# Up product of the ConvFFN without plain pairs: two products of 16 pairs run first, in PSUM banks of their own

## The chip, the cores and the metric

One core of a Trainium2 chip runs one layer of a streaming encoder in one launch. The metric is the device time of that launch in microseconds, as the median of three runs. The clock that was granted to TensorE in the profiled execution is 0.997 of full speed, so throttling plays no part here.

## The reference, cut to what matters

The layer handles T = 1056 tokens (1024 of a prompt and 32 of a decode group) at D_MODEL = 1024, with D_FF = 2816. The part that matters is the ConvFFN and the product just ahead of it:

```python
mix = (sigmoid(ga) * (oa @ w_br_a) + sigmoid(gb) * (ob @ w_br_b)) @ w_out
x = x + rms_norm(mix, g_post_mix)
f, conv_new = conv_ffn(rms_norm(x, g_pre_ffn), ...)

def conv_ffn(h, conv_s0, w_up, conv_w, conv_b, w_down):
    a, g = jnp.split(h @ w_up, [D_FF], axis=-1)             # w_up: 1024 x 5632
    gx = jnp.concatenate([conv_s0, g], axis=1)
    gc = conv_b + sum(conv_w[i] * gx[:, i:i + T] for i in range(3))
    return (gelu(gc) * a) @ w_down, gx[:, T:]
```

All arithmetic is float32.

## The kernel before, in words

Features lie on the 128 partitions and tokens along the free axis, so an activation of 1024 features is eight slices of 128. A float32 product is made of three matmuls in a faster format (fp32r in the names): each factor is split into a high half, copied by ScalarE (whi, mh/hh), and a low half, that is the factor less its high half, made by VectorE (wlo, ml/hl). High times high, high times low and low times high are added in PSUM. Raw weights are loaded by DMA on SP's queue; results go out by POOL's queue.

**Order.** From the out product to the end of the plain pairs the code stands in a `manual_schedule`: PE, DVE and ACT issue their work as it is written. Behind it a scheduler chooses the order by data and buffers; weights (`plus`, `weight`) have high priority there. Each engine works its queue in order.

**PSUM.** `repsum((mm, one, two))` deals the eight banks out: so many single banks called mm, so many called one, so many pairs of banks called two. The call ahead of the branch products deals (4, 4, 0), and this holds for the stages branch (L1653 and on: L1664 reads a product into ev, with the low half oa3l of an activation made at L236 by VectorE), out and plain up. The next call, (0, 0, 4), holds for the pairs that take seven products.

**Out and norm.** The product with w_out goes over three chunks of 352 tokens, eight slices each. ScalarE squares and scales each slice (sq, z), VectorE sums the squares (accz, L1866). `norm_steps` is a generator that does the norm of a chunk: fold accz (L1744) and split it into two halves y (L1755, L1756), sum over partitions by TensorE, inverse root by VectorE, scale z (L1778), add the residual, and do the same once more for the norm ahead of the up product (L1781 scales z, L1810 makes the low half in ml/hl, and the rows are also stored in DRAM as d_hn). The numbers in OUT_STEPS and UP_STEPS say how many steps of the generator stand behind each product. The norm of chunk 2, the last, is spread over the up product that follows.

**Up.** The 44 slices of w_up are 22 pairs (f), of a slice of a and one of g. Pairs 0 to 3 are plain: two halves by three chunks by 24 matmuls of 352 columns (L230 to L232). Each of the other 18 takes a 2x2 scheme with seven products in place of eight: features and tokens are halved (528 tokens a half, one and two), the two slices of the weights make the other way to halve, and a product is 24 matmuls of 264 columns (L2048 to L2050) into a pair of banks. In the order of the program, with tN the differences of quarters of the activation, sN those of weights:

```python
X  = a11*b11 -> p1 (ScalarE, L2065)     Y = s2*t2      -> c12 = p1 + Y (L2103)
Z  = s1*t1   -> q = p1 + Z (L2107)      X += a12*b21   -> c11 (ScalarE, L2109)
Y += s3*t3   -> last quarter = q + Y (L2058 to L2060)
Z += s4*b22  -> c12 += Z (L2115)        Y += a22*t4    -> c21 = p1 + Y (L2117)
```

`plus` (L2031) makes the weight sums ws, `weight` their halves (L2038, L2039). The quarters t1 to t4 are made during the plain pairs and after (`quarter_sums`, `quarter_third`, `quarter_last`) from rows of d_hn that are read back, t2 by way of DRAM.

**Behind a pair.** `activate` does the convolution (L1899 on ScalarE, L1901 and L1902 on VectorE, in the single buffer gc), gelu (L1906), the product with a (L1911, L1913, into av), and sm, the sum of both token halves (L1921), which it puts in gc. POOL stores av and sm in d_b for the down product; from pair 11 on these stores accumulate. The last pair (21) runs its products in another order. The down product (L2510 to L2512) follows.

Of the kernel before, what the change touches and what calls it, by code (L numbers as in the profile page):

```python
# [1 line left out]

# [94 lines left out]
UP_PLAIN = 4  # L97

THIRD = ((0, 0), (1, 0, 0), (0, 1, 0), (0, 0, 1), (1,), ())
# [4 lines left out]
OUT_STEPS = (1, 1, 1, 2, 2, 2, 2, 1)  # L104
UP_STEPS = (0, 1, 2, 2, 2, 1, 2, 2, 2)
# [8 lines left out]
def emit(tc, a):  # L114
# [1525 lines left out]
    repsum((MODE, 8 - MODE, 0))  # L1640
# [108 lines left out]
    def norm_steps(tmp, c, z, acc, g, resid, keep, g_next, dst, spill=None):  # L1749
# [58 lines left out]
        def low_half(i):  # L1808
            nh, nl = dst(i)
            ve.tensor_tensor(nl, zs[i], nh, op=ALU.subtract)  # L1810

        for i in range(KT // 2):
            times(i, g_next, rstd(s))
            if spill is not None:
                po.dma_start(both(spill, i), zs[i])
            ac.activation(dst(i)[0], zs[i], AF.Copy)
            if i:
                low_half(i - 1)
            yield
# [17 lines left out]
    wup = {}  # L1837

    def up_weights(f, j):
        n = f + FT * (1 - j)  # L1840
        wup[f, j] = weights(a["w_up"][n], ve) if f == 0 else split_into(uw, a["w_up"][n], 8)
# [3 lines left out]
    for c in range(NC):  # L1845
# [3 lines left out]
        for n in range(KT):  # L1849
# [3 lines left out]
            if c == 0:  # L1853
                out_weights(n + 2)
            else:
                norm_part(OUT_STEPS[n])
            if c == NC - 1 and n in (4, 5):
                up_weights(0, n - 4)
# [8 lines left out]
        if c == 0:  # L1867
# [3 lines left out]
                          lambda i, s=s: [t[:, 2 * i : 2 * i + 2, s] for t in (hh, hl)], d_hn)  # L1871
        next(norm)
        for i in rest or ():
            pass
# [20 lines left out]
    def activate_steps(f, gx, av):  # L1895
# [24 lines left out]
        both, sm = av.rearrange("p (q t) -> p q t", q=2), gc[:, :HT]  # L1920
# [10 lines left out]
    def plain_out(gx, av, j, s, ps):  # L1931
        if j:
            ac.activation(av[:, s], ps, AF.Copy)
        elif s.stop <= NP:
            ac.activation(gx[:, s.start + 2 : s.stop + 2], ps, AF.Copy)
        else:
            n = NP - s.start
            ac.activation(gx[:, s.start + 2 : NP + 2], ps[:, :n], AF.Copy)
            ac.activation(gx[:, NP + 4 :], ps[:, n:], AF.Copy)

    def up_plain():
        bufs = {}
        steps = [(0, 0, 0), (0, 1, 0), (0, 0, 1), (0, 1, 1)]
        steps += [(f, j, c) for cs in ((0, 1), (2,)) for f in range(3) for j in range(2) for c in cs if f or c == 2]

        for i, (f, j, c) in enumerate(steps):
            if (f, 0) not in bufs:
                bufs[f, 0] = up_buffers(f)
            gx, av = bufs[f, 0]
            s = chunk(c)  # L1950
            ps = ps_mm()[:, : s.stop - s.start]
            hi, lo = wup[f, j]
            product(ps, hi, lo, [(k, k) for k in range(KT)], lambda k: hh[:, k, s], lambda k: hl[:, k, s])
            if i == 14:
                wup[3, 0] = weights(a["w_up"][3 + FT], ve)
            if i < 9:
                norm_part(UP_STEPS[i])
            elif i >= 11:
                next(rest, None)
            if i % 2 == 0 and 1 + i // 4 < 3:  # L1960
                up_weights(1 + i // 4, i // 2 % 2)
            if i == 8:
                rest = plain_rest(bufs)
            plain_out(gx, av, j, s, ps)
        return bufs


    XS = {}
    d_t2 = tl(dram, [HK, P, HT], tag="d_t2")

    def quarter_rows(k):
        b = [tl(sh, [P, T], tag="hn", bufs=2) for i in range(2)]
        dma.dma_start(b[0], d_hn[k])
        dma.dma_start(b[1][:, two], d_hn[k + HK, :, two])
        return b[0][:, one], b[0][:, two], b[1][:, two]

    def quarter_split(n, k, t):
        h, l = (v[:, k] for v in XS[n])
        ac.activation(h, t, AF.Copy)
        ve.tensor_tensor(l, t, h, op=ALU.subtract)  # L1980

    def quarter_sums():
        for n in ("t1", "t2"):
            XS[n] = [tl(sp, [P, HK, HT], F32R, tag=n + x, bufs=1) for x in "hl"]
        for k in range(HK):
            b11, b12, b22 = quarter_rows(k)
            t1, t2 = [tl(sh, [P, HT], tag="xs", bufs=2) for i in range(2)]
            ve.tensor_tensor(t1, b12, b11, op=ALU.subtract)
            ve.tensor_tensor(t2, b22, t1, op=ALU.subtract)
            dma.dma_start(d_t2[k], t2)  # L1990
            quarter_split("t1", k, t1)
            quarter_split("t2", k, t2)
            yield

    def quarter_third():
        XS["t3"] = [tl(sw, [P, HK, HT], F32R, tag="t3" + x) for x in "hl"]
        for k in range(HK):
            t = tl(sh, [P, T], tag="hn", bufs=2)
            dma.dma_start(t[:, one], d_hn[k, :, two])
            dma.dma_start(t[:, two], d_hn[HK + k, :, two])  # L2000
            yield
            ve.tensor_tensor(t[:, one], t[:, two], t[:, one], op=ALU.subtract)
            quarter_split("t3", k, t[:, one])
            yield

    def quarter_last():
        XS["b11"] = [t[:, up1, one] for t in (hh, hl)]
        XS["b21"] = [t[:, up2, one] for t in (hh, hl)]
        XS["b22"] = [t[:, up2, two] for t in (hh, hl)]
        XS["t4"] = [t[:, up1, two] for t in (hh, hl)]  # L2010
        for k in range(HK):
            t = tl(sh, [P, T], tag="hn", bufs=2)
            dma.dma_start(t[:, one], d_t2[k])
            dma.dma_start(t[:, two], d_hn[HK + k, :, one])
            ve.tensor_tensor(t[:, one], t[:, two], t[:, one], op=ALU.subtract)
            quarter_split("t4", k, t[:, one])
# [4 lines left out]
    def up_strassen(f):  # L2021
        raw = [tl(wp, [P, KT, P], tag="raw", bufs=2), tl(wp, [P, KT, P], tag="raw", bufs=2) if f == UP_PLAIN else sw_raw()[:, : KT * P].rearrange("p (k c) -> p k c", c=P)]
# [5 lines left out]
        def plus(x, y, o, e):  # L2028
            t = tl(sw, [P, HK, P], tag="ws", bufs=3)
# [32 lines left out]
        X = ps_pair()  # L2062
        X_ = X[:, :, :HC]
        mul(X, weight(a11, WL_ENG[0]), "b11", True, True)
        ac.activation(p1, X_, AF.Copy)  # L2065
# [37 lines left out]
        ve.tensor_tensor(c12, p1, Y_, op=ALU.add)  # L2103
        Z = ps_pair()
# [3 lines left out]
        mul(X, weight(a12, WL_ENG[3]), "b21", False, True)  # L2108
        ac.activation(c11, X_, AF.Copy)  # L2109
# [10 lines left out]
    sp = sh = None  # L2120


    def plain_rest(bufs):
        nonlocal sp, sh
        zp.release()
        sp = pool("sp", side="right")
        for x in ("t1h", "t1l", "t2h", "t2l"):
            tl(sp, [P, HK, HT], F32R, tag=x, bufs=1)
        sh = pool("sh", side="right")
        yield from quarter_sums()  # L2130
        activate(0, *bufs[0, 0])
        yield
# [706 lines left out]
```

## Time and profile before

| | |
|---|---|
| median of 3 runs | 1900.38 us (1898.66 to 1902.38) |
| the profiled execution: span | 1898.7 us; no other time is shown for it |
| TensorE matmul (PE), weight load (PEld) | 1864.9 us (98%), 1828.7 us (96%) |
| VectorE (DVE) | 1232.9 us (65%) |
| ScalarE (ACT) | 956.5 us (50%) |
| GpSimd (POOL) | 211.6 us (11%) |
| memory traffic | 166 GB/s over the span |

All views come from one profiled execution. Times are microseconds from the start of the span. In a list by time a row gives start, duration, engine, line, operation, output and inputs, sizes, and in brackets how long the engine stood idle ahead of it and what released it. In a table of stretches each engine has its busy time and its count of instructions. In a list by group "573/578/584" are the shortest, mean and longest duration in nanoseconds, followed by the time of the first and the last. In a list of transfers a row ends with the KB of one and the median time from issue to landing. TensorE's matmuls are pipelined, so that their durations overlap.

### The profile page before, as it was taken

To read this page: it belongs to the slowest core of one execution; us is meant where nothing else is said; L and a number is where in the kernel's file an instruction comes from. 1 tells how busy PE (TensorE), PEld (TensorE's weight loads), DVE (VectorE), ACT (ScalarE), POOL (GpSimd) and SP (SyncE) were. 2 spreads that over 40 slices of the span, in tenths; PEclk is the share of its full clock that TensorE was granted. 3 is DMA by queue.
4 is the path that set the end of the run, shared out by engine and by line. 5 is a ranking of instruction groups with operands and counts; after the bars stand their busy time and mean duration, and the time that the engine had idled before them with its cause. 6 is when DMAs were issued, how large, how long until landed. Compare 5 with 4: busy or idle time off the path is not lost.

```text
span 1898.7 us, 34427 instructions
## 1 busy us (share of the span) xinstructions
PE 1864.9 (98%) x13616; PEld 1828.7 (96%) x13616; DVE 1232.9 (65%) x2325; ACT 956.5 (50%) x2028; POOL 211.6 (11%) x374
## 2 busy tenths in 40 slices
PE   8999999999999999999999999999999999999996
PEld 8999999999999999999999999999999999999996
DVE  6955544566655766675544776777776775558776
ACT  7545335666666676563324544443433344555555
POOL 0000001010000111011210121111122110000112
PEclk9999999999999999999999999999999999999998
DMA  7223326233315656678633446334445468987646
GB/s 282 82 101 108 108 82 195 66 98 85 103 49 143 164 150 172 180 225 284 232 114 116 145 154 217 135 133 140 138 109 133 109 188 295 299 276 240 235 147 109
DMA packets 112702, 300.89 MB, mean 158 GB/s; under 512 B 12756, under 2 KB 36636, under 8 KB 111900
## 3 DMA queue, kind: packets, MB, share of 16 engines
q1 hardware_dynamic: 83084, 205.95, 34.0%
q0 software_dynamic: 28016, 88.05, 17.1%
q10 hardware_dynamic: 1440, 4.69, 0.6%
q8 instruction: 107, 1.75, 0.4%
q14 instruction: 55, 0.45, 0.1%
HBM read 201.20 MB, written 114.09 MB: 166 GB/s over the span
## 4 chain that ended last, share of the span: by engine, by line
PE 84%; DVE 6%; ACT 5%; DMA 3%; issue 2%; POOL 0%; SPq 0%; ACTq 0%; DVEq 0%; POOLq 0%
PE two L2048 6%; PE mm L232 6%; PE mm L230 6%; PE two L2049 6%; PE two L2050 6%; PE mm L231 6%; PE mm L821 5%; PE mm L823 5%; PE mm L822 5%; PE two L618 4%; PE two L619 4%; PE two L620 4%; PE two L2511 3%; PE two L2512 3%; PE two L2510 3%
## 5 line engine op out<-in xcount | busy, mean ns | idle before, releaser
L821 PE MATMUL mm<-xh,whi 128*128 128x352 f32 x696 | 238.1, 342 | 0.4 <-ACT ev L714 0.4
L823 PE MATMUL mm<-xh,wlo 128*128 128x352 f32 x696 | 225.1, 323 | 0.0
L822 PE MATMUL mm<-xl,whi 128*128 128x352 f32 x696 | 224.6, 323 | 0.0
L2512 PE MATMUL two<-d,wlo 128*128 128x264 f32 x616 | 175.4, 285 | 0.8 <-DVE wlo L2247 0.8
L2511 PE MATMUL two<-d,whi 128*128 128x264 f32 x616 | 174.9, 284 | 0.9 <-DVE d L2198 0.8
L2510 PE MATMUL two<-d,whi 128*128 128x264 f32 x616 | 174.4, 283 | 0.0
L2050 PE MATMUL two<-mh,wlo 128*128 128x264 f32 x576 | 163.3, 285 | 0.0
L2048 PE MATMUL two<-mh,whi 128*128 128x264 f32 x576 | 161.7, 285 | 1.5 <-DVE gx L2060 1.5
L2049 PE MATMUL two<-ml,whi 128*128 128x264 f32 x576 | 163.0, 284 | 0.0
L821 PEld LDWEIGHTS mm<-xh,whi 128*128 128x128 f32 x696 | 131.2, 189 | 3.2 <-ACT ev L714 0.7
L822 PEld LDWEIGHTS mm<-xl,whi 128*128 128x128 f32 x696 | 131.3, 189 | 0.3
L823 PEld LDWEIGHTS mm<-xh,wlo 128*128 128x128 f32 x696 | 130.6, 188 | 0.0
L2511 PEld LDWEIGHTS two<-d,whi 128*128 128x128 f32 x616 | 115.9, 188 | 1.5 <-DVE d L2198 1.5
L2512 PEld LDWEIGHTS two<-d,wlo 128*128 128x128 f32 x616 | 115.6, 188 | 1.0 <-DVE wlo L2247 1.0
L2510 PEld LDWEIGHTS two<-d,whi 128*128 128x128 f32 x616 | 116.3, 189 | 0.0
L2048 PEld LDWEIGHTS two<-mh,whi 128*128 128x128 f32 x576 | 107.5, 188 | 1.7 <-DVE gx L2060 1.7
L2050 PEld LDWEIGHTS two<-mh,wlo 128*128 128x128 f32 x576 | 108.5, 188 | 0.2 <-DVE wlo L2039 0.2
L2049 PEld LDWEIGHTS two<-ml,whi 128*128 128x128 f32 x576 | 108.4, 188 | 0.0
L958 ACT ACTIVATE s<-s,sm 128x640 f32<-128x640 f32 (+5 forms) x72 | 50.6, 703 | 93.4 <-DVE sm L957 93.4
L618 PE MATMUL two<-th,whi 128*128 128x264 f32 x320 | 90.8, 284 | 0.0
L619 PE MATMUL two<-tl,whi 128*128 128x264 f32 x320 | 90.8, 284 | 0.0
L620 PE MATMUL two<-th,wlo 128*128 128x264 f32 x320 | 90.6, 284 | 0.0
(630 smaller groups left out, 5870.7 us busy)
## 6 DMA issues: line engine op xcount, KB each, us to landing
raw<-in_w_in SPq DMA_DIRECT2D x52, 512.0 KB, 3.7
d_b<-av POOLq DMA_DIRECT2D x33, 528.0 KB, 4.2
d_ws<-in_w_down POOLq DMA_DIRECT2D x24, 704.0 KB, 6.5
uraw<-d_b SPq DMA_DIRECT2D x32, 528.0 KB, 5.7
raw<-in_w_up SPq DMA_DIRECT2D x27, 512.0 KB, 3.6
wraw<-d_ws SPq DMA_DIRECT2D x16, 704.0 KB, 5.6
d_b<-gc POOLq DMA_DIRECT2D x11, 792.0 KB, 5.8
sraw<-in_w_up SPq DMA_DIRECT2D x17, 512.0 KB, 4.6
```

Source lines behind the costliest of these rows:

```text
L618: pe.matmul(ps[:, j, :HC], w[0][:, k], x[0](k, s), start=st, stop=False, skip_group_check=True)
L619: pe.matmul(ps[:, j, :HC], w[0][:, k], x[1](k, s), start=False, stop=False, skip_group_check=True)
L620: pe.matmul(ps[:, j, :HC], w[1][:, k], x[0](k, s), start=False, stop=sp_, skip_group_check=True)
L821: pe.matmul(ps, wh, h[:, k, s], start=(k == 0), stop=False)
L822: pe.matmul(ps, wh, l[:, k, s], start=False, stop=False)
L823: pe.matmul(ps, wl, h[:, k, s], start=False, stop=(k == cnt - 1))
L2048: pe.matmul(ps[:, j, :HC], w[0][:, k], x[0][:, k, s], start=st, stop=False, skip_group_check=True)
L2049: pe.matmul(ps[:, j, :HC], w[0][:, k], x[1][:, k, s], start=False, stop=False, skip_group_check=True)
L2050: pe.matmul(ps[:, j, :HC], w[1][:, k], x[0][:, k, s], start=False, stop=sp_, skip_group_check=True)
L2510: pe.matmul(o, wh, xh_[:, s], start=(k == 0 and p in (0, 4, 5)), stop=False, skip_group_check=True)
L2511: pe.matmul(o, wh, xl_[:, s], start=False, stop=False, skip_group_check=True)
L2512: pe.matmul(o, wl, xh_[:, s], start=False, stop=(k == HD - 1 and p in (3, 4, 6)), skip_group_check=True)
```

## The change

- No pair is plain any more; all 22 take seven products.
- For 16 pairs (AHEAD) the two products that go into X run in a stage of their own, ahead of all others: `up_ahead` makes a11\*b11, copies it to av as p1 (L2013), adds a12\*b21 in the same bank, copies that as c11, and POOL stores both in DRAM (d_e). Later `up_strassen` reads p1 and c11 back (SP's queue) and does the other five products. Pairs 4, 8, 12, 16, 20 and 21 do all seven there.
- The first four products of each kind in this stage are cut at the half of the tokens' half (264 columns), so that they can start before the norm of chunk 2 is done; `norm_steps` of chunks 1 and 2 run on behind them, with new OUT_STEPS and UP_STEPS.
- PSUM is dealt (3, 1, 2) from the branch products on, in place of (4, 4, 0): two pairs of banks for the new stage, and single banks for its first products.
- The high and low halves of the activation are only made for what the scheme uses (`used`).
- Rows of d_hn for the quarters t1 to t4 are loaded straight into the tiles that will hold their low halves (tXl) and summed from there during the new stage (`quarter_sums`, L1972 on ScalarE); t2 no longer goes by DRAM.
- sm has a tile of its own (L1941, one buffer), except for the last pair. p1 has two buffers in place of one.
- Raw weights of the new stage lie in the buffers raw and gx (`up_load`, `up_split`).

```diff
-UP_PLAIN = 4
+AHEAD = (0, 1, 2, 3, 5, 6, 7, 9, 10, 11, 13, 14, 15, 17, 18, 19)
-UP_STEPS = (0, 1, 2, 2, 2, 1, 2, 2, 2)
+UP_STEPS = (1, 1, 1, 1, 0, 1, 0, 1) + (1,) * 12
...
-    repsum((MODE, 8 - MODE, 0))
+    repsum((3, 1, 2))
...
-        both, sm = av.rearrange("p (q t) -> p q t", q=2), gc[:, :HT]
+        both, sm = ..., gc[:, :HT] if f == FT - 1 else tl(sw, [P, HT], tag="sm", bufs=1)
...
+    def ahead_product(X, i, p, js=(0, 1)):
+        h, l = wup[i, p]
+        xh_, xl_ = [t[:, p * HK : p * HK + HK] for t in (hh, hl)]
+        for j in js:
+            o, t = (X[j] if isinstance(X, list) else X[:, j])[:, :HC], slice(j * HC, (j + 1) * HC)
+            for k in range(HK):
+                pe.matmul(o, h[:, k], xh_[:, k, t], start=(p == 0 and k == 0), stop=False, ...)
+                pe.matmul(o, h[:, k], xl_[:, k, t], start=False, stop=False, ...)
+                pe.matmul(o, l[:, k], xh_[:, k, t], start=False, stop=(k == HK - 1), ...)
...
+        def store(i):
+            po.dma_start(d_e[i], av.pop(i))
...
+        def step(i, p, js, after=()):
+            if i not in X:
+                X[i] = ps_pair() if i > 1 else [ps_mm(), ps_mm()] if i == 0 else [ps_mm(), ps_pair()[:, 0]]
+                av[i] = tl(fp, [P, T], tag="av", bufs=3)
+            ahead_product(X[i], i, p, js)
+            for f in done:
+                f()
+            done[:] = [lambda: ahead_out(X[i], av[i], p, js), *after]
...
+        for g in range(2, n, 2):
+            for p in range(2):
+                for i in (g, g + 1):
+                    more = [lambda i=i, p=p: up_split(i + 2, p)]
+                    if p:
+                        more += [lambda i=i: up_load(i + 5), lambda i=i: store(i)]
+                    step(i, p, (0, 1), more)
...
-        p1 = v2(tl(sw, [P, HT], tag="p1", bufs=1))
+        p1 = v2(p1_tiles(1)[0])
+        ahead = f in AHEAD
+        if ahead:
+            dma.dma_start(p1, v2(d_e[AHEAD.index(f), :, two]))
...
-        mul(X, weight(a11, WL_ENG[0]), "b11", True, True)
-        ac.activation(p1, X_, AF.Copy)
+        if not ahead:
+            X = ps_pair()
+            X_ = X[:, :, :HC]
+            mul(X, weight(a11, WL_ENG[0]), "b11", True, True)
+            ac.activation(p1, X_, AF.Copy)
...
         ve.tensor_tensor(c12, p1, Y_, op=ALU.add)
+        if ahead:
+            dma.dma_start(c11, v2(d_e[AHEAD.index(f), :, one]))
...
-    for f in range(UP_PLAIN, FT):
+    for f in range(FT):
         last_up = up_strassen(f)
```

In the lists of order that follow, a row is the line, the operation, and output<-inputs with their number and shape; all are rows of one engine's queue, in order. First VectorE in a pair of seven products before (av takes c12, c is q, and the rows L1901 to L1921 belong to the pair ahead):

```order
L2103 TENSOR_TENSOR av_14730<-p_2165_14733,two_14769 128x528
L2039 TENSOR_TENSOR wlo_14894<-ws_14891,whi_14893 128x512
L2031 TENSOR_TENSOR ws_15097<-raw_14964,sraw_14965 128x512
L2107 TENSOR_TENSOR c_2166_14734<-p_2165_14733,two_14799 128x528
L2039 TENSOR_TENSOR wlo_14923<-sraw_14726,whi_14922 128x512
L1901 SCALAR_TENSOR_TENSOR gc_14712<-gx_14490,vec_69,gc_14712 128x1058
L2039 TENSOR_TENSOR wlo_14976<-raw_14964,whi_14975 128x512
L1902 SCALAR_TENSOR_TENSOR gc_14712<-gx_14490,vec_69,gc_14712 128x1058
L2058 TENSOR_TENSOR gx_14729<-c_2166_14734,two_14769 128x264
L2059 TENSOR_TENSOR gx_14729<-c_2166_14734,two_14769 128x232
L2060 TENSOR_TENSOR gx_14729<-c_2166_14734,two_14769 128x32
```

The same engine after, in a pair of five products (L2154 is c12, L2160 is q, L2108 to L2110 the last quarter):

```order
L2154 TENSOR_TENSOR av_13867<-p_2071_13870,two_13877 128x528
L1921 SCALAR_TENSOR_TENSOR gc_13848<-gx_13683,vec_69,gc_13848 128x1058
L2086 TENSOR_TENSOR wlo_14003<-sraw_13863,whi_14002 128x512
L1922 SCALAR_TENSOR_TENSOR gc_13848<-gx_13683,vec_69,gc_13848 128x1058
L2160 TENSOR_TENSOR c_2072_13871<-p_2071_13870,two_13908 128x528
L2086 TENSOR_TENSOR wlo_14062<-ws_14058,whi_14061 128x512
L1933 TENSOR_TENSOR av_13684<-gc_13848,av_13684 128x528
L1931 SCALAR_TENSOR_TENSOR av_13684<-gc_13848,av_13684 128x496
L1931 SCALAR_TENSOR_TENSOR av_13684<-gc_13848,av_13684 128x32
L2108 TENSOR_TENSOR gx_13866<-c_2072_13871,two_13877 128x264
L2109 TENSOR_TENSOR gx_13866<-c_2072_13871,two_13877 128x232
L2110 TENSOR_TENSOR gx_13866<-c_2072_13871,two_13877 128x32
```

The convolution of the pair ahead moved in front of q, and the product with a in front of the last quarter.

VectorE where the out product ends, before (accz is the sum of squares of chunk 2, y one half of its fold, z_11695 the chunk ahead of it):

```order
L1810 TENSOR_TENSOR ml_10552<-z_11695,mh_10551 128x2x352
L1781 SCALAR_TENSOR_TENSOR z_11695<-z_11695,vec_69,rstd_8_84 128x352 x2
L1810 TENSOR_TENSOR ml_10552<-z_11695,mh_10551 128x2x352
L1866 TENSOR_TENSOR accz_12002<-accz_12002,sq_12272 128x704
L1744 TENSOR_TENSOR accz_12002<-accz_12002 128x352
L1756 TENSOR_TENSOR y_1876_12318<-accz_12002,y_1875_12317 128x352
```

And after:

```order
L1882 TENSOR_TENSOR accz_12002<-accz_12002,sq_12267 128x704
L1780 SCALAR_TENSOR_TENSOR z_11695<-z_11695,vec_69,rstd_8_84 128x352 x2
L1811 TENSOR_TENSOR ml_10552<-z_11695,mh_10551 128x2x176
L1780 SCALAR_TENSOR_TENSOR z_11695<-z_11695,vec_69,rstd_8_84 128x352 x2
L1811 TENSOR_TENSOR ml_10552<-z_11695,mh_10551 128x2x352 x2
L235 TENSOR_TENSOR wlo_12384<-gx_12309,whi_12383 128x512
L1743 TENSOR_TENSOR accz_12002<-accz_12002 128x352
L1755 TENSOR_TENSOR y_1889_12397<-accz_12002,y_1888_12396 128x352
```

The last addition to accz moved ahead of four scalings and three low halves of the chunk ahead; the fold and y stay behind them and a weight's low half.

Last, ScalarE where the new stage ends, after (av are the copies of the stage's products, t1h to t4 in mh the high halves of the quarters, whi those of the first weights of pair 0):

```order
L1972 ACTIVATE t1h_12952<-p_2014_13417 128x528
L1972 ACTIVATE t3h_12950<-p_2015_13418 128x528
L2013 ACTIVATE av_13355<-two_13354 128x528
L1972 ACTIVATE t2h_12954<-c_2016_13419 128x528
L1972 ACTIVATE mh_10551<-ws_13420 128x528
L2085 ACTIVATE whi_13512<-ws_13509 128x512
L2085 ACTIVATE whi_13543<-ws_13507 128x512
L2013 ACTIVATE av_13391<-two_13390 128x528
```

The quarters' last high halves stand between the copies of the last two products of the stage; before, the same copies stood among those of pair 3 (L1979, L1935) and the first weights.

More of the change, by code (lines that the diff above doesn't have):

```diff
@@ L1 @@
 import contextlib
+import itertools
 import numpy as np
@@ L1928, in activate_steps @@
             to(sm, slice(3, 4), accum_op=ALU.add)
[L1931 to L1965, printed above, removed]
@@ L1995, in quarter_third @@
[L1995 to L2006, printed above, removed]
+    d_e = tl(dram, [len(AHEAD), P, T], tag="d_e")
```

195 lines of the change are left out of this document (118 added, 77 removed).

## The prediction

> **What bounds the kernel now.** I read the page's busy times first, then the stretches of the three stages the change touches, then TensorE's and VectorE's instructions in order of time there.
>
> ```profile
> PE 1864.9 (98%) x13616; PEld 1828.7 (96%) x13616; DVE 1232.9 (65%) x2325; ACT 956.5 (50%) x2028; POOL 211.6 (11%) x374
> PE 84%; DVE 6%; ACT 5%; DMA 3%; issue 2%; POOL 0%; SPq 0%; ACTq 0%; DVEq 0%; POOLq 0%
> ...
> core 0: us, PE busy (x) PEld busy (x) DVE busy (x) ACT busy (x) POOL busy (x), PEclk, DMA share, GB/s
> 1092.00:1186.00 94.00, 94.00 (x581) 94.00 (x580) 65.80 (x98) 43.29 (x81) 15.89 (x31) 1.00 0.55 186
> 1186.00:1556.00 370.00, 368.53 (x3023) 368.14 (x3022) 271.98 (x437) 146.41 (x211) 63.15 (x117) 1.00 0.47 133
> 1580.00:1700.00 120.00, 120.00 (x990) 120.00 (x990) 64.69 (x83) 62.54 (x98) 9.00 (x13) 1.00 0.89 292
> ```
>
> TensorE is busy 98% of the span, and the chain that ended last runs through it for 84%. In the stretch of the plain pairs (1092 to 1186) it never idles; in that of the seven-product pairs (1186 to 1556) it idles 1.5 us in 370, at full clock. So here a matmul removed is time removed, as long as VectorE (272 of 370 us busy) and the transfers keep up with a faster pace. The third stretch is a later one, kept for what it says of DMA load.
>
> **The matmuls.** Their price is the distance from the first of a kind to the first of the next.
>
> ```profile
> 1091.90 0.32 PE L230 MATMUL mm<-mh,whi 128*128 128x352 f32 x1
> ...
> 1186.01 0.28 PE L2048 MATMUL two<-mh,whi 128*128 128x264 f32 x1
> ...
> 1328.62 0.39 PE L2048 MATMUL two<-mh,whi 128*128 128x264 f32 x1 [1.47 <-DVE gx L2060]
> ...
> 1556.39 0.28 PE L2510 MATMUL two<-d,whi 128*128 128x264 f32 x1
> ```
>
> The 0.28 and 0.32 us are pipelined durations that overlap; the starts count. Four plain pairs are 4 x 2 halves x 3 chunks x 24 = 576 matmuls of 352 columns, plus four for norms: 94.11 us / 580 = 0.1623 us. Eighteen pairs are 18 x 7 x 24 = 3024 of 264 columns: (370.38 - 1.47) / 3024 = 0.1220 us, so a product of 24 takes 2.93 us. Afterwards all 22 pairs take seven products: 672 matmuls of 264 replace 576 of 352, 82.0 us for 93.5: **-11.5 us**. That two of the seven are now done early for 16 pairs adds no matmul.
>
> Per column the rows give 0.461 ns at 352 and 0.462 at 264: shortening costs nearly nothing here. The Trainium skill says, in "Perfetto Trace Analysis", section "Optimizing Tensor Performance", that larger matmuls are more efficient where possible, which speaks against 672 small ones. "TensorE: Matmul & The Clock Gate" (section "Wait — 56ns, not 53.3ns?") prices one at N / 2.4 GHz plus about 2.5 ns; by it the sum, an estimate, would be 10.3 instead of 11.5 us. The measured starts decide.
>
> **The stall that was there.** The one wait of 1.47 us above has its cause three queues back.
>
> ```profile
> 1318.57 0.77 POOL L1918 DMA_DIRECT2D d_b<-gc  x1 [1.95 <-ACT whi L2038]
> ...
> 1323.36 1.27 ACT L1899 ACTIVATE gc<-gx,vec 128x1058 f32<-128x1058 f32 x1 [5.07 <-DMA d_b<-gc]
> 1324.53 0.62 ACT L2038 ACTIVATE whi<-raw 128x512 fp32r<-128x512 f32 x1
> 1325.05 0.59 ACT L2109 ACTIVATE av<-two 128x528 f32<-128x528 f32 x1
> 1327.86 1.09 ACT L1906 ACTIVATE gc<-gc 128x1058 f32<-128x1058 f32 x1 [2.21 <-DVE gc L1902]
> ...
> 1327.73 0.42 DVE L2058 TENSOR_TENSOR gx<-c,two 128x264 f32<-128x264 f32 x1
> 1328.07 0.39 DVE L2059 TENSOR_TENSOR gx<-c,two 128x232 f32<-128x232 f32 x1
> 1328.38 0.18 DVE L2060 TENSOR_TENSOR gx<-c,two 128x32 f32<-128x32 f32 x1
> ```
>
> The half sum sm sits in the single gc buffer, and the next pair's convolution may not start on ScalarE until the store of sm has left it; VectorE's three rows that read t3's product stand behind that convolution. The change gives sm a tile of its own (L1941), so this wait goes: **-1.5 us**. Next late would be the single sm tile: its store is issued about 9.5 us into a pair's frame, and with the slowest landing row below (7.9 us) it is free 17.4 us in, before the next sm at 14.6 + 8.6.
>
> ```profile
> sraw<-in_w_up SPq DMA_DIRECT2D x15, 512.0 KB, 4.6
> ...
> d_b<-gc POOLq DMA_DIRECT2D x10, 264.0 KB, 7.9
> ```
>
> **VectorE in a five-product pair.** Now it has 14.64 us per pair instead of 20.5.
>
> ```profile
> 1311.13 1.31 DVE L1902 SCALAR_TENSOR_TENSOR gc<-gx,vec,gc 128x1058 f32<-128x1058 f32 x1
> 1312.36 0.69 DVE L2115 TENSOR_TENSOR av<-av,two 128x528 f32<-128x528 f32 x1
> 1312.98 0.68 DVE L2039 TENSOR_TENSOR wlo<-ws,whi 128x512 fp32r<-128x512 f32 x1
> 1313.60 0.71 DVE L1913 TENSOR_TENSOR av<-gc,av 128x528 f32<-128x528 f32 x1
> 1314.23 0.67 DVE L1911 SCALAR_TENSOR_TENSOR av<-gc,av 128x496 f32<-128x496 f32 x1
> 1314.81 0.68 DVE L2031 TENSOR_TENSOR ws<-raw,ws 128x512 f32<-128x512 f32 x1
> 1315.42 0.18 DVE L1911 SCALAR_TENSOR_TENSOR av<-gc,av 128x32 f32<-128x32 f32 x1
> 1315.52 0.70 DVE L2117 TENSOR_TENSOR gx<-p,two 128x528 f32<-128x528 f32 x1
> 1316.13 0.68 DVE L2039 TENSOR_TENSOR wlo<-raw,whi 128x512 fp32r<-128x512 f32 x1
> 1316.73 0.68 DVE L2031 TENSOR_TENSOR ws<-sraw 128x512 f32<-128x512 f32 x1
> 1317.34 0.70 DVE L1921 TENSOR_TENSOR gc<-av 128x528 f32<-128x528 f32 x1
> ```
>
> From start to start: 0.62 for 528 elements, 0.60 to 0.62 for 512, 1.23 for 1058. A short pair has five low halves (3.0), four weight sums (2.4), four sums of products (2.5), the three rows of the last quarter (0.8), two convolution steps (2.5), three gelu products (1.3) and sm (0.6): 13.1 us, 89% of 14.64. A walk along the new order, zero where t2's product ends: c12 (L2154) at 0 to 0.9, needed before t3 starts at 2.9; q (L2160) after two convolution steps and a low half, at 3.9 to 4.6, needed when b22 starts at 6.1 (t3 and two matmuls of the next pair later); the last quarter (L2108 to L2110) after gelu, at 6.6 to 7.4, needed by t4 at 10.6; c12 again at 9.2 when b22 is done; c21 (L2171) waits for t4's end at 13.6 although VectorE is free from 11.7. ScalarE's rows for the same pair (five high halves of 0.63, convolution 1.27, gelu 1.09) are 5.5 us. So each deadline is met by 1.5 us or more and 2 us per pair stay free; a full pair (4, 8, 12, 16, 20, 21) gives 5 us more. Steady cost: none, with VectorE's own queue as cover. Bounds for the 16 short pairs: nothing, and one wait of 1.47 us in each, 23.5 us, if the cover is gone. The walk is nearer to nothing; I take one such wait, as many as before: **+1.5 us**.
>
> **Three banks instead of four.** The call ahead of the branch products now asks for three mm banks (it was four), so a product may start only when the one three before it has been read.
>
> ```profile
> 890.17 0.53 DVE L1664 TENSOR_TENSOR ev<-mm,ev 128x352 f32<-128x352 f32 x1 [1.42 <-PE mm L232]
> 895.08 1.26 DVE L236 TENSOR_TENSOR oa3l<-ev,oa3h 128x1056 fp32r<-128x1056 f32 x1 [4.38 <-ACT oa3h L235]
> 896.25 1.38 DVE L1664 TENSOR_TENSOR ev<-mm,ev 128x352 f32<-128x352 f32 x3
> ...
> 905.51 0.32 PE L230 MATMUL mm<-oa0h,whi 128*128 128x352 f32 x1
> ```
>
> Twelve products of 12 matmuls (1.94 us) end at 905.51, so the fifth ended near 892.0, and VectorE, held by oa3l, read it only at 896.25 to 896.7, with the sixth and seventh. The eighth wants to start at 895.8: with four banks it may, with three it waits: **+0.9 us**. From then on TensorE has no slack, so it stays in the end. The long products behind read within 0.3 us; nothing more there.
>
> **The seam from out to up.** The chunk-2 sum (accz) and its halves now stand behind more work on VectorE.
>
> ```profile
> 1094.70 0.89 DVE L1866 TENSOR_TENSOR accz<-accz,sq 128x704 f32<-128x704 f32 x1 [0.41 <-ACT sq L1861]
> 1095.62 0.53 DVE L1744 TENSOR_TENSOR accz<-accz 128x352 f32<-128x352 f32 x1
> 1096.78 0.53 DVE L1756 TENSOR_TENSOR y<-accz,y 128x352 fp32r<-128x352 f32 x1 [0.62 <-ACT y L1755]
> ...
> L1781 DVE SCALAR_TENSOR_TENSOR z<-z,vec,rstd x24: 573/578/584, 1056.4 to 1130.5; 128x352 f32<-128x352 f32 x24
> L1810 DVE TENSOR_TENSOR ml<-z,mh x12: 880/884/893, 1058.4 to 1132.0; 128x704 fp32r<-128x704 f32 x12
> ```
>
> Now accz comes about 1.2 us earlier (ScalarE's two copies ahead are half as wide), but four scalings of z, three low halves and a weight's low half (4.9 us) stand between it and y, which lands 9.2 us after the last out product. TensorE reaches the norm's two matmuls after six half products, 8.8 us: **+0.4 us**, bounds 0 and 1.5 (the wait of the stage). Behind it every step is 2.9 us, and VectorE's share of one at most 2.4 us (a weight's low half, and two rows over z as wide as the 0.89 us row).
>
> **The seam to the short pairs.** After the last-but-one ahead product ScalarE copies it (0.6, like av above), splits t2 and t4 (0.6 each), then whi of the first weight (0.6), and VectorE its low half (0.6): 3.2 us for the 2.9 of the last product, **+0.3 us**, bounds 0 and 1.5. Before, the sums were finished under the first short products.
>
> Added transfers: 16 stores to d_e by POOL and 32 loads by SP, a second read of 16 weight tiles. SP queues c11's load behind the store that frees av, and the next sraw behind that; both are issued by 3 us into a frame and sraw is needed at 10.5, against 4.6 to land. A short pair moves 133 GB/s x 20.6 us = 2.74 MB plus 0.54, 223 GB/s; the last stretch above carries 292 GB/s with TensorE 100% busy. Cost: none.
>
> Sum: -11.5 - 1.5 + 1.5 + 0.9 + 0.4 + 0.3 = **-9.9 us** on an execution of 1898.7 us (the span; nothing is shown around it), so 1888.8. The median of the runs is 1.7 us above that span: **1890.5 us** to be measured.
>
> **Rivals.** *VectorE becomes the bound.* If rows cost their recorded duration, a short pair is 5 x 0.68 + 4 x 0.69 + 4 x 0.70 + 0.99 + 2.62 + 1.56 + 0.70 = 14.8 us against 14.64, and what it cannot fill comes on top: 0.15 to 0.4 us a pair, 1893 to 1897. The Trainium skill has the rule for that: in "VectorE: DVE Perf Modes", section "The DRAIN you can't avoid", the next operation does not start until the pipe is empty. The rows above start 0.07 before the one ahead has ended, so the trace speaks against it: 14%.
>
> *Slower: the queue gets stuck in every short pair.* The wait of 1.47 us was VectorE's in-order queue held by one late row. Short pairs have fewer products between t3 and t4 and share one sm tile and two p1 tiles with loads. If each of 16 sticks once, 23.5 us less the 1.5 counted turn -9.9 into +12.1: 1912. It decides from 11.4 / 16 = 0.7 us per pair. For it: 89% load; against it: the 1.5 us margins. 12%.
>
> *Gain lost to late loads.* Four or five p1, c11 or weight loads that land late by one such wait each, in the crowded stretch where rows of d_hn, weights and d_e move together: 1896 to 1899, no change. 9%.
>
> **How the numbers follow.** Forecast 65%, with its own range 1887 (all gains, no cost) to 1893. About 0.2% (3.8 us) is what a measurement of this kernel tells from no change. Faster: forecast and first rival, 0.79. Same: 0.09. Slower: 0.12. The range 1887 to 1900 leaves out the slower rival.
>
> **What would show it.** Right: 3696 matmuls of 264 columns at 0.122 us; no wait on the d_b store at the convolution; one wait near 0.9 us on VectorE before the eighth branch product; VectorE near 90% busy between the seams with TensorE idle under 3 us there. Wrong: repeated waits of t3, b22 or t4 on VectorE's rows L2154, L2160, L2110, or of c12 on a load of p1; then the time is 1896 or more.

## The result and the profile after

The changed kernel takes 1887.72 us (median of 4 runs, 1885.08 to 1888.09), the kernel before 1900.49 us (4 runs, 1898.66 to 1902.38). The ratio is 0.9931, with a 95% interval of 0.9912 to 0.995. A second comparison, on another occasion, gave 1886.94 us (6 runs) against 1901.0 us (23 runs), 0.9916 (0.9896 to 0.9935). The change saves 13 to 14 us; 9.9 us were predicted.

The profiled execution after has a span of 1883.4 us. These are the busy times and the chain of work that ended last on its page.

```profile
PE 1851.6 (98%) x13712; PEld 1815.8 (96%) x13712; DVE 1259.5 (67%) x2379; ACT 957.0 (51%) x2022; POOL 220.1 (12%) x390
...
PE 82%; DVE 6%; ACT 5%; DMA 4%; issue 2%; SPq 0%; ACTq 0%; DVEq 0%
```

And these the stretches of the changed stage, cut at 1241 us, in the columns of the prediction's table of stretches:

```profile
1091.20:1241.00 149.80, 149.75 (x1233) 149.54 (x1232) 114.61 (x185) 74.34 (x127) 26.61 (x52) 1.00 0.66 233
1241.00:1541.40 300.40, 300.40 (x2473) 300.40 (x2472) 250.04 (x405) 116.16 (x158) 61.46 (x114) 1.00 0.61 177
```

TensorE idles 0.05 us in 450 us. VectorE is busy 250 of 300 us in the second stretch; it was 272 of 370.

The rows below are TensorE's in order of time: the first product of the new stage, the first of the short pairs, the first of the down product, and between them three places that the prediction priced.

```profile
895.10 0.43 PE L229 MATMUL mm<-bh,whi 128*128 128x352 f32 x1 [0.87 <-DVE ev L1663]
...
1091.31 0.28 PE L2004 MATMUL mm<-mh,whi 128*128 128x264 f32 x1
...
1100.10 0.33 PE L1760 MATMUL one<-y,onesDr 128*128 128x352 f32 x1
1100.43 0.28 PE L2004 MATMUL mm<-mh,whi 128*128 128x264 f32 x1
...
1185.07 0.28 PE L2095 MATMUL two<-t2h,whi 128*128 128x264 f32 x1
1185.52 0.39 PE L2097 MATMUL two<-t2h,wlo 128*128 128x264 f32 x1
...
1541.38 0.28 PE L2540 MATMUL two<-d,whi 128*128 128x264 f32 x1
```

From the first up product to the first down product it took 1556.39 - 1091.90 = 464.49 us before and takes 1541.38 - 1091.31 = 450.07 us now, 14.4 us less. This stretch is the measure for everything below, because it hardly varies: three more profiles of kernels with the same code there gave 93.76 and 356.31 us, 450.07 together, each time. The total varies by some 5 us, since the first up product starts anywhere from 1090.3 to 1096.1 us (in every profile but the one with copies, below), mostly by waits in stages that the change leaves alone.

### The profile page after: what moved, and what is told of

Same layout as the page of the kernel before. It is cut to its first block, busy times and chain, and to the rows that moved or that the text cites. A ratio compares the mean times of both kernels' runs of the same rounds, so it can differ in the third digit from the quotient of the medians.

```text
span 1883.4 us, 34773 instructions
## 1 busy us (share of the span) xinstructions
PE 1851.6 (98%) x13712; PEld 1815.8 (96%) x13712; DVE 1259.5 (67%) x2379; ACT 957.0 (51%) x2022; POOL 220.1 (12%) x390
## 3 DMA queue, kind: packets, MB, share of 16 engines
q0 software_dynamic: 30320, 96.70, 18.4%
## 4 chain that ended last, share of the span: by engine, by line
PE 82%; DVE 6%; ACT 5%; DMA 4%; issue 2%; SPq 0%; ACTq 0%; DVEq 0%
PE two L2097 6%; PE two L2095 6%; PE two L2096 6%; PE mm L820 5%; PE mm L822 5%; PE mm L821 5%; PE mm L229 5%; PE mm L231 4%; PE mm L230 4%; PE two L617 4%; PE two L618 4%; PE two L619 4%; PE two L2542 3%; PE two L2541 3%; PE two L2540 3%
## 5 line engine op out<-in xcount | busy, mean ns | idle before, releaser
L2085 ACT ACTIVATE whi<-ws 128x512 fp32r<-128x512 f32 x88 | 55.4, 630 | 161.8 <-PE two L2096 160.8
L2096 PE MATMUL two<-ml,whi 128*128 128x264 f32 x448 | 126.7, 284 | 0.0
L2097 PE MATMUL two<-mh,wlo 128*128 128x264 f32 x448 | 126.3, 284 | 0.0
L2095 PE MATMUL two<-mh,whi 128*128 128x264 f32 x448 | 126.0, 284 | 0.0
L235 DVE TENSOR_TENSOR wlo<-raw,whi 128x512 fp32r<-128x512 f32 x80 | 55.7, 700 | 56.7 <-ACT whi L234 56.2
L2276 DVE TENSOR_TENSOR wlo<-wraw,whi 128x512 fp32r<-128x512 f32 (+1 forms) x81 | 51.8, 645 | 51.3 <-ACT whi L2275 51.1
```

Of the source, the lines that this page charges most:

```text
L2095: pe.matmul(ps[:, j, :HC], w[0][:, k], x[0][:, k, s], start=st, stop=False, skip_group_check=True)
L2096: pe.matmul(ps[:, j, :HC], w[0][:, k], x[1][:, k, s], start=False, stop=False, skip_group_check=True)
L2097: pe.matmul(ps[:, j, :HC], w[1][:, k], x[0][:, k, s], start=False, stop=sp_, skip_group_check=True)
```

## The experiments

The stretch, in two parts (up to the first product with t2, and from there to the first down product), in every profile, with the waits of TensorE that the second part lists:

| kernel | first part | second part | together | listed waits |
|---|---|---|---|---|
| before | 94.11 | 370.38 | 464.49 | 1.5 |
| before, profiled again | 94.12 | 369.30 | 463.42 | 0.6 |
| before, sm in its own tile | 94.11 | 369.60 | 463.71 | 0.8 |
| after; again; four mm banks; copies beside | 93.76 | 356.31 | 450.07 | none |
| after, sm in gc | 93.76 | 374.76 | 468.52 | 12.4 |
| after, two more rows of VectorE | 93.76 | 356.60 | 450.36 | none |
| after, four more rows | 93.75 | 380.63 | 474.38 | 14.2 |
| after, weights loaded twice | 93.75 | 363.77 | 457.52 | 4.9 |
| after, 12 pairs ahead | 85.89 (15.2 of it a wait) | 382.55 | 468.44 | none |
| after, 20 pairs ahead | 117.01 | 332.50 | 449.51 | none |
| after, 20 ahead, four mm banks | 117.01 | 332.49 | 449.50 | none |

**The changed kernel again** (no edit).

> The changed kernel unaltered, timed in five rounds beside the kernel before, as the base for the variants of it. If the gain is as the first runs and the two traces have it (464.5 us from the first up product to the first down product before, 450.1 after, 0.9 us lost at the branch products), the difference is 12 to 14 us (1886.5 to 1888.5). If the first difference of 12.8 us was partly luck of the runs, it comes out near the 9.9 us that were predicted (1890.5).

1886.94 us; ratio to the kernel before 0.9916 (0.9896 to 0.9935). The gain of 13 to 14 us stands. In this profile the eighth branch product did not wait. TensorE had lost 1.3 us at an earlier wait; that this is why is not shown, since with the weights loaded twice (below) it lost 2.7 us there and still waited 0.6 us.

**The stall alone, taken out of the kernel before.**

```diff
-        both, sm = ..., gc[:, :HT]
+        both, sm = ..., tl(sx, [P, HT], tag="sm", bufs=1) if 2 <= f < FT - 1 else gc[:, :HT]
```

> The kernel before with one edit: sm gets a tile of its own for the pairs of seven products (all but the last). Theory: the one wait of t4 on VectorE's L2060 goes, and with it 1.5 us (or 1.8, counting the three matmuls beside it that ran 0.1 us late): some 1898.7, and TensorE's idle time in that stretch 0. Rival: the wait was one of several that hide behind each other, another takes its place and the time stays at 1900.4. If the sm tile were the main part of the gain, the time would fall by 5 us or more.

1900.56 us against 1901.0; ratio 0.9993 (0.9979 to 1.0008), no change that shows in the total. The wait on L2060 is gone, and TensorE's list of waits names another, on ScalarE's copy of p1:

```profile
1238.93 0.39 PE L2048 MATMUL two<-mh,whi 128*128 128x264 f32 x1 [0.84 <-ACT p L2065]
```

So part of the rival came true, and what the tile saved here is 370.38 - 369.60 = 0.8 us at most; against the second profile of the kernel before (369.30, next run) it saved nothing. The gain of the change is not the tile's alone.

**The kernel before, profiled again** (no edit).

> The kernel before, unaltered, profiled a second time. Theory: the wait of t4 on VectorE's L2060 is a matter of where the stores of sm land, so it comes in some runs and pairs and not in others; the seven-product stretch (370.38 us in the first profile, 369.60 with sm in a tile of its own) lies between 368.5, which is 18 times the undisturbed pair of 20.475 us, and 372. Rival: the wait is fixed by the order and comes again at the same pair with 1.5 us (370.4).

TensorE's row at the product that waited before:

```profile
1326.56 0.39 PE L2048 MATMUL two<-mh,whi 128*128 128x264 f32 x1 [0.62 <-DVE gx L2060]
```

The place was the same both times, the size was not: 0.6 us here, 1.5 us in the first profile. The store of sm just ahead landed 4.7 us after its issue both times; here it was issued 1.05 us earlier, counted from the first up product. Most of that lead arose two pairs ahead, where the store of sm landed after 5.8 us in place of 6.5. Late landings carry over from pair to pair.

**Four mm banks in the changed kernel.**

```diff
-    repsum((3, 1, 2))
+    repsum((4, 0, 2))
-            ps = ps_one()[:, :CW]
+            ps = ps_mm()[:, :CW]
```

> The changed kernel with banks (4, 0, 2) in place of (3, 1, 2): four mm banks as before the change, the norm takes its bank from them too. Theory: the wait of the eighth branch product on VectorE's L1663 (0.87 us in the trace after) is gone, TensorE never idles before the norm's matmuls, and the time falls by 0.9 us against the changed kernel (about 1886.9). Rival: the product waits for the weight or for the activation's low half a moment later, so that less than 0.3 us is gained; or the norm, which now takes turns with products for a bank, waits in the out product and the gain is lost.

1887.47 us (6 runs) beside 1886.94 for the changed kernel: not to be told apart. In the traces it can be: no wait on L1663. Of the nine profiles with three banks, six show it, 0.3 to 1.4 us long; of the five with four banks, none. The wait is real, as predicted, about 0.6 us on average, and too small for totals.

**sm back in gc.**

```diff
-        both, sm = ..., gc[:, :HT] if f == FT - 1 else tl(sw, [P, HT], tag="sm", bufs=1)
+        both, sm = ..., gc[:, :HT]
```

> The changed kernel with sm back in the convolution's buffer gc, as before the change. In the trace after, the convolution of the next pair starts 3.8 to 5.5 us after the store of sm is issued, and that store takes 4.3 to 11.1 us to land (median 7.2). Theory (the sticking queue is real, and only the tile of its own keeps it away): the convolution comes 2 to 3 us late in most of the 16 short pairs, VectorE's rows behind it up to 1.5 us too late for the banks, +8 to +25 us against the changed kernel (1896 to 1912), with waits of b22, t3 or t4 on VectorE. Rival (VectorE's slack of 1.7 us per pair takes it up): within 1.5 us of the changed kernel, and the tile was worth no more than the 1.5 us of the one wait before.

1904.51 us (12 runs), ratio to the kernel before 1.002 (1.0004 to 1.0036): slower than before the change, and 17.6 us above the changed kernel. The chain of one such wait, in rows of ScalarE, VectorE and TensorE in order of time:

```profile
1475.09 1.27 ACT L1919 ACTIVATE gc<-gx,vec 128x1058 f32<-128x1058 f32 x1 [5.00 <-DMA d_b<-gc]
1476.39 1.32 DVE L1921 SCALAR_TENSOR_TENSOR gc<-gx,vec,gc 128x1058 f32<-128x1058 f32 x1 [4.21 <-ACT gc L1919]
1477.63 0.70 DVE L2154 TENSOR_TENSOR av<-p,two 128x528 f32<-128x528 f32 x1
1478.47 0.36 PE L2095 MATMUL two<-t3h,whi 128*128 128x264 f32 x1 [3.64 <-DVE av L2154]
```

And the lists of waits of ScalarE and TensorE over the seven-product stretch (total us, times, longest):

```profile
ACT gc L1919 <- DMA d_b<-gc: 49.5, 17, 5.4
...
PE two L2095 <- DVE c L2160: 6.7, 6, 2.1
PE two L2095 <- DVE av L2154: 4.2, 2, 3.6
```

c12 (L2154) needs nothing of the convolution; it stands behind L1921 in VectorE's queue, and t3 waits for it. 17 convolutions are late by 49.5 us, of which VectorE's slack takes up most; 12.4 us arrive at TensorE, and the stretch grows by 18.5 us. This is the mechanism of the prediction's slower rival, and what keeps it away is one line of the change.

**More VectorE work per pair.** The row that makes sm is issued three times, and in the next kernel five times.

```diff
+        for i in range(3 if f < FT - 1 else 1):
             ve.tensor_tensor(sm, av[:, one], av[:, two], op=ALU.add)
```

> The changed kernel with VectorE's row that makes sm issued three times in place of once in every pair but the last (same output; 1.24 us more of VectorE per pair by starts 0.62 apart). Read by the stretch from the first up product to the first down product, 450.07 us in three profiles so far. Theory (a row costs the distance between starts; 13.1 of 14.57 us are used in a short pair, 1.5 free): within 1 us of 450.1. Rival (a row costs its recorded 0.70 us and VectorE is full at 14.8 us): the 16 short pairs grow by 1.2 to 1.4 us each, 470 us.

> As the run with two more rows, but four more rows of sm in every pair but the last: 2.48 us more of VectorE, 1.0 us over what is free in a short pair. Theory: VectorE is the bound in the 16 short pairs, each grows by 1.0 us, less what the full pairs between them (7 us free) and the 1.5 us of slack of each run of short pairs take up: 458 to 466 us for the stretch, with waits of b22, t3 and t4 on VectorE. Rival of full recorded durations: 490 us. If the slack were larger than the walk says: 450 still.

Two more rows (1.24 us by starts) cost 0.3 us in 21 pairs. VectorE's list of waits tells where the time came from. Its wait for TensorE at c21 in the changed kernel,

```profile
DVE gx L2171 <- PE two L2097: 25.5, 21, 1.8
```

and with two more rows,

```profile
DVE gx L2172 <- PE two L2098: 12.3, 15, 2.1
```

Its idle time shrank, TensorE's did not grow. Rows cost the distance of their starts here, not their recorded durations, and the rival in which VectorE becomes the bound falls. The section of the Trainium skill that the prediction sets beside that rival ("VectorE: DVE Perf Modes", "The DRAIN you can't avoid") goes on to say that a next op that is not held starts earlier. The starts 0.07 us before the recorded end agree with that part. Four more rows (2.48 us) cost 24.3 us, between what the two theories expected. The dose did more than it was meant to: it also delays the store of sm, and the next pair's first row of sm waits for that store, as VectorE's list of waits shows:

```profile
DVE sm L1942 <- DMA d_b<-sm: 26.9, 9, 8.2
```

TensorE's first four waits in the second part, 3.2 us together, end at 1353.8 us, before the first of these waits for the store ends at 1357.3 us, so the store has no part in them. How the rest of the 24.3 us divides between VectorE's work and the single sm tile stays open. The free time per short pair lies between 1.2 and 2.5 us. Behind the stretch the last row of sm waits 8.2 us for the store and TensorE then 7.4 us for VectorE, so the whole kernel (1920.99 us, one run) is 34 us above the changed one.

**20 pairs ahead, and 12.**

```diff
-AHEAD = (0, 1, 2, 3, 5, 6, 7, 9, 10, 11, 13, 14, 15, 17, 18, 19)
+AHEAD = tuple(range(20))
```

> The changed kernel with 20 pairs ahead in place of 16 (pairs 0 to 19; only 20 and 21 do all seven products), so that no full pair gives VectorE a rest among the short ones. The count of matmuls is the same. Theory (each short pair fits by itself): 449.5 to 450.5 us for the stretch. Rival (the full pairs at every fourth place take up a backlog of VectorE or of the loads): waits grow towards the end of the 20, 452 us or more.

449.51 us, no wait: each short pair fits by itself, and the full pairs at every fourth place are not needed as a rest. With 12 pairs (0 to 3, 5 to 7, 9 to 11, 13, 14):

> The changed kernel with 12 pairs ahead in place of 16, so that the stage has 28 steps in place of 36, and 9 steps of the quarter sums are left over at its end with no product beside them. The count of matmuls is the same. Theory (the stage must be long enough to cover the norm and the sums): 13 us of VectorE work less one product of 2.9 us that is still beside it, so TensorE waits some 8 to 12 us at the seam to the short pairs and the stretch takes 458 to 463 us. Rival (the sums slip in beside the first products): under 453 us.

468.44 us for the stretch, above the range of the theory: the wait was longer than expected, and the clock fell behind it. TensorE's row:

```profile
1181.11 0.59 PE L2095 MATMUL two<-t2h,whi 128*128 128x264 f32 x1 [15.22 <-ACT whi L2085]
```

The stretches around it, with the granted clock as the third number from the end:

```profile
1165.90:1181.10 15.20, 0.00 (x0) 0.00 (x0) 13.90 (x23) 8.51 (x15) 0.53 (x1) 0.63 0.21 74
1181.10:1185.00 3.90, 3.89 (x16) 3.61 (x17) 3.87 (x7) 1.73 (x3) 0.00 (x0) 0.50 0.09 33
1185.00:1190.00 5.00, 5.00 (x35) 5.00 (x35) 3.07 (x5) 0.63 (x1) 0.00 (x0) 0.80 0.55 173
1190.00:1200.00 10.00, 10.00 (x85) 10.00 (x84) 6.80 (x13) 2.53 (x4) 0.80 (x2) 1.00 0.32 100
```

VectorE works 13.9 of the 15.2 us that TensorE stands still: the leftover quarter sums, with nothing beside them. The granted clock is 0.50 for 3.9 us behind the wait and 0.80 over the next 5, which is half clock for some 5.9 us in all and costs about 2.9 us, an estimate; the wait and this make up nearly all of the 18.4 us by which the stretch is longer. The length of the new stage is what pays for them, so 16 pairs is not an idle choice; 12 are too few.

**More transfers.**

```diff
         for r, n in zip(raw, (f, FT + f)):
-            dma.dma_start(r, a["w_up"][n])
+            for i in range(2 if f in AHEAD else 1):
+                dma.dma_start(r, a["w_up"][n])
```

> The changed kernel with both raw weight tiles of each of the 16 short pairs loaded twice into the same tile (1.05 MB more per pair, some 250 GB/s in place of 177 over the stretch). Theory (transfers are hidden; the stage behind it moves 269 GB/s with TensorE at 99%): 450 to 451 us for the stretch. Rival (the loads of p1 and c11 behind them on SP's queue, or the weights, land late): waits of c12 on p1, of the convolution on c11, or of the weights' halves on the load, 1.5 us each, 455 to 470 us.

The stretch is 457.52 us: the rival. In the lists of waits of SP's queue and of VectorE, a load of a tile is held until the load of the same tile ahead of it has landed, and the weight sums then wait for it:

```profile
SPq L2072 <- DMA raw<-in_w_up: 60.0, 14, 6.0
SPq L2072 <- DMA sraw<-in_w_up: 54.8, 14, 5.9
...
DVE ws L2079 <- DMA sraw<-in_w_up: 21.9, 11, 6.1
```

c12 stands behind such a sum, and TensorE's row waits for c12:

```profile
1473.05 0.36 PE L2096 MATMUL two<-t3h,whi 128*128 128x264 f32 x1 [2.77 <-DVE av L2155]
```

14 times 4.3 us for one tile and 14 times 3.9 us for the other: the second loads came one landing late, and 11 times a weight sum waited for that. So where it did, the loads of the changed kernel have about 4 us to spare at most. One landing itself took hardly longer. The rows of the lists of transfers, first of the changed kernel, then of this one:

```profile
raw<-in_w_up SPq DMA_DIRECT2D x20, 512.0 KB, 4.4
sraw<-in_w_up SPq DMA_DIRECT2D x20, 512.0 KB, 3.6
...
raw<-in_w_up SPq DMA_DIRECT2D x34, 512.0 KB, 3.9
sraw<-in_w_up SPq DMA_DIRECT2D x34, 512.0 KB, 4.2
```

The medians went from 4.4 to 3.9 us and from 3.6 to 4.2, at 212 GB/s in place of 175; some 250 had been expected. To tell the delay from shared bandwidth, the next kernel copied as much from memory to memory:

```diff
             dma.dma_start(p1, v2(d_e[AHEAD.index(f), :, two]))
+            dma.dma_start(d_x[AHEAD.index(f)], a["w_up"][f])
```

> The changed kernel with a copy of 0.5 MB from memory to memory on SP's queue in each of the 16 short pairs, which nothing waits for (1.05 MB of traffic more per pair, about as much as with the weights loaded twice, but no load comes later in its queue than by the issue). If the 7.4 us of the run with double loads came from the second load landing after the first (4 us late), the stretch stays at 450 to 451 us. If they came from shared bandwidth, it is 455 to 460.

It does not answer the question, though the stretch is 450.07 us. Nothing made a copy wait, so the scheduler put all 16 at the start of the program. The row of the copies, with their first and last start behind the durations:

```profile
L2107 SPq DMA_DIRECT2D d_x<-in_w_up x16: 488/488/602, 16.2 to 44.0; - x16
```

The first 100 us of this kernel in the table of stretches,

```profile
0.00:100.00 100.00, 82.70 (x533) 78.81 (x534) 64.46 (x82) 54.52 (x91) 1.96 (x9) 0.91 0.66 247
```

and of the changed kernel:

```profile
0.00:100.00 100.00, 92.29 (x664) 88.96 (x665) 77.82 (x100) 60.49 (x100) 2.70 (x10) 1.00 0.49 177
```

There they compete with the first loads: 533 matmuls get done in place of 664. The 19 us by which this kernel (1906.6 us) is slower than the changed one were lost ahead of the change, whose first product starts at 1111.68 us. So no run separates delay from bandwidth for the double loads. SP's list and the landings of the weights, longer by 0.6 us at most in the median, speak for the delay; the stores of av, which took 5.3 us in the median in place of 3.6, leave bandwidth a part.

**Both edits that seemed to help.** 20 pairs ahead and four mm banks together:

> The two edits that the runs so far speak for, together: 20 pairs ahead (449.51 us for the stretch against 450.07) and four mm banks (no wait of the eighth branch product, 0.6 to 1.4 us in five of seven profiles with three banks). Expected against the changed kernel: 0.6 us less in the stretch and up to 1 us less at the branch products, 1885.5 to 1887, which is within what a comparison of totals tells apart; against the kernel before 14 to 15.5 us less.

1888.08 us (6 runs), ratio to the kernel before 0.9937 (0.9918 to 0.9955): no better than the changed kernel in the total. The stretch is 449.50 us, 0.6 us less; the start of the up product, 1093.56 us in this profile, varies by more.

## Why the prediction was right

The direction and the place were right, and the time lies in the range, at its lower edge: 1887.72 us, and 1886.94 in the second comparison, where the forecast's own range began at 1887 for all gains and no cost. The gain came out 3 to 4 us larger than the sum, because no step came out worse than its term and most came out better. Step by step:

- **Matmuls, -11.5 us: right in kind, 1.1 us too small.** Two rows of the kernel before, nine undisturbed pairs apart, give its true rate:

```profile
1349.32 0.28 PE L2049 MATMUL two<-ml,whi 128*128 128x264 f32 x1
...
1533.58 0.28 PE L2049 MATMUL two<-ml,whi 128*128 128x264 f32 x1
```

  That is 184.26 / 9 = 20.473 us a pair, so 18 pairs are 368.5 us and the stretch without the stall is 462.6 us; 450.07 is 12.55 less, with the 0.3 us lost at the seam already in it. The products became a little cheaper as well: the new stage's 32 take 93.76 us less 0.65 for the norm, 2.91 each, where a full pair's average 2.925.
- **The stall, -1.5 us.** It cost 370.38 - 368.5 = 1.9 us in the first profile and 0.8 in the second. The prediction took the listed wait and charged what followed it to the matmuls' rate.
- **One wait assumed among the short pairs, +1.5 us: this is the term that failed.** None came, in any profile with sm in its own tile and the transfers and VectorE's work unchanged. The walk had said so, and its order holds in the trace. VectorE's rows c12, q and the end of the last quarter in one short pair, and the starts of t3, b22 and t4, which need them:

```profile
1396.55 0.70 DVE L2154 TENSOR_TENSOR av<-p,two 128x528 f32<-128x528 f32 x1
1398.99 0.70 DVE L2160 TENSOR_TENSOR c<-p,two 128x528 f32<-128x528 f32 x1
1402.20 0.18 DVE L2110 TENSOR_TENSOR gx<-c,two 128x32 f32<-128x32 f32 x1
...
1398.33 0.28 PE L2095 MATMUL two<-t3h,whi 128*128 128x264 f32 x1
1401.50 0.28 PE L2095 MATMUL two<-mh,whi 128*128 128x264 f32 x1
1405.39 0.28 PE L2095 MATMUL two<-mh,whi 128*128 128x264 f32 x1
```

  The margins are 1.1, 1.8 and 3.0 us. Over all 16 short pairs the smallest are 1.1, 1.3 and 1.7 us, so the walk's "1.5 us or more" was somewhat too generous (it had 2.0 for c12), but every deadline was met. A term put in against the walk, only because there had been a wait before, was caution and not a reading.
- **Three banks, +0.9 us.** 0.87 us in the trace after, at the product that was named; 0.6 on average over the profiles with three banks.
- **The seam from out to up, +0.4 us: nothing.** The 0.45 us between the product ahead and that at 1100.43 is the norm's two matmuls (0.33) and one step of 0.12.
- **The seam to the short pairs, +0.3 us.** The third matmul of the first short product comes 0.2 us late and the one behind it 0.1: 0.3 us.
- **Transfers, 0.** Right, with less to spare than the 292 GB/s row suggested: with the weights loaded twice the stretch lost 7.4 us at 212 GB/s, most likely by the moment of landing. The second stretch after moved 177 GB/s, where a short pair had been put at 223.

Together the steps give some 13 to 14 us, which fits the 12.8 and 14.1 us of the two comparisons. Of the signs that the prediction named, TensorE's idle time, the wait before the eighth branch product and the absence of waits in the short pairs came as said; VectorE was busy 83% of the second stretch, not near 90%.

The slower rival was right in kind, and too dear: where sm goes back to gc, the queue sticks and the kernel is 3.5 us slower than before, 18.5 us more in the stretch where the rival had 23.5. That it did not come with the change is due to sm's own tile, as the prediction had argued for the one stall it found.

## What to carry to other kernels

Where TensorE is busy 98% of the time, count matmuls and columns first, then look for the buffer that a slow store holds while an in-order queue stands behind it: here one buffer of 528 columns, worth 0.8 us at most in the kernel before, was worth 18.5 us in the changed one, more than the 12.6 us of matmuls that the change saved. If a pair is shortened, that buffer has to be freed sooner too, and a wait that cost TensorE 1.5 us once in 18 pairs can come 11 times. Compare the length of the stage that was changed, by the starts of its first and last rows, not the totals: the stage repeated to 0.01 us where the total moved by 5.

## What the runs showed of the hardware

A wait of TensorE can cost more than it lasts. The second part grew by 0.8 us for 0.6 of listed waits (before, again), 1.9 for 1.5, 7.5 for 4.9, 18.5 for 12.4 and 24.3 for 14.2. A small part is how waits are counted: a listed wait starts at the recorded end of the matmul ahead, which lasts 0.28 us where starts lie 0.12 us apart, so by starts each costs 0.16 us more. In the kernel with four more rows of VectorE the granted clock (third number from the end) shows a larger part. Its row behind two waits of 0.6 and 1.78 us,

```profile
1353.78 0.39 PE L2096 MATMUL two<-mh,whi 128*128 128x264 f32 x1 [1.78 <-DVE c L2161]
```

and the stretches that follow:

```profile
1353.70:1355.00 1.30, 1.22 (x7) 1.22 (x8) 1.30 (x4) 0.00 (x0) 0.00 (x0) 0.68 1.02 401
1355.00:1357.00 2.00, 2.00 (x11) 2.00 (x11) 1.17 (x1) 0.79 (x1) 0.22 (x2) 0.50 0.65 264
1357.00:1359.00 2.00, 2.00 (x16) 2.00 (x16) 1.17 (x2) 0.82 (x2) 0.00 (x0) 0.86 0.03 8
1359.00:1361.00 2.00, 2.00 (x18) 2.00 (x18) 2.00 (x5) 0.11 (x1) 0.00 (x0) 1.00 0.01 4
```

The clock falls to half for some 3.4 us and then returns; that costs about 1.7 us more, an estimate from these rows. It does so four times in the stretch of this kernel (6.8 us), once with sm in gc and once with the weights loaded twice (1.7 us each); up to 2.6 us of an excess stay unexplained. Single waits up to 2.1 us left it at 1.00, single waits of 2.7 us and longer, and these two close together, did not. After 15.2 us of standing still it was half for some 5.9 us of work. The Trainium skill, in "TensorE: Matmul & The Clock Gate", section "Part 1: The HAM clock gate (the "warmup" mystery)", says that TensorE runs at half its clock after at least one idle window of about 3.4 us and at full clock after about as long of steady work. The time to return agrees behind the short waits (3.4 us) and was longer behind the long one (5.9 us); the fall came here after waits shorter than that window.
